# Gate chunks of the second block's modulation computed in the first block's layers

## Chip, cores and metric

One core of a Trainium2 chip runs the whole program. The metric is the device time of one execution in microseconds (us), the median of several runs; less is better.

## What is computed

The reference sends 256 tokens of width 1024 through two layers of a first block (five attention-like branches and an output product each), a final norm, and then one second block. The second block is modulated by a conditioning vector `c`:

```python
def second_block(x, c, w_ada, b_ada, ...):
    c_act = jax.nn.silu(c)
    ada = c_act @ w_ada[l] + b_ada[l]
    shift_a, scale_a, gate_a, shift_m, scale_m, gate_m = jnp.split(ada, N_ADA, axis=-1)
    h = modulate(rmsnorm(x, g_mix[l]), shift_a, scale_a)
    proj = h @ w_in[l]
    ...
    y = jnp.concatenate([o_gla, o_moba], axis=-1) @ w_out[l]
    x = x + gate_a[:, None, :] * y
    h = modulate(rmsnorm(x, g_mlp[l]), shift_m, scale_m)
    x = x + gate_m[:, None, :] * (jnp.square(jax.nn.relu(h @ w_ff1[l])) @ w_ff2[l])
    return rmsnorm(x, g_final)
```

`ada` has 6144 columns, which the kernel computes as 12 chunks of 512: chunks 0 to 3 are shift and scale of the mixers (GLA and MoBA), 4 and 5 the gate `gate_a`, 6 to 9 shift and scale of the MLP, 10 and 11 `gate_m`. They need only `c`, no token.

## The kernel before

All weights are streamed once, in pieces of up to [128, 4, 512] f32 (1 MB). `run_stream` walks the list of pieces: a piece is loaded 6 ahead on SP's queue into one of three raw buffers (L393), split 3 ahead into a rounded high part on ACT (`wh`, L408) and the rest on DVE (`wl`, L409), each with four buffers, and multiplied on TensorE (PE) as three products high × high, low × high, high × low: L470, L471 and L473 for a token-major result, L493, L495 and L496 for a transposed one. The raw buffer is free again when the L409 of its piece has read it.

A chunk of `ada` is two pieces of `w_ada` that are not split (`raw`). DVE alone multiplies and adds them up: for each of the eight rows of the chunk one instruction, L1403 the first and L1405 the other seven, on 128x512. Then `fin` splits the sum (L1414 on ACT, L1415 on DVE), PE sums over partitions with a matrix of ones (L1419, L1420), and either ACT copies one row (L1423), which POOL's queue sends to the array `adaR`, or, for a gate, POOL's queue loads `b_ada` on all partitions (L1430) and DVE adds (L1431). `spread` sorts the chunks' pieces evenly between the other pieces: chunks 0 to 3 in the first layer, 6 to 9 in the second (table `ADA`), 4 and 5 in the second block from its fifth piece on, 10 and 11 in the MLP.

The order on each engine is that of the program, where generators ("lanes") and deferred steps are woven between the chunks of the stream; `behind(mark)` puts an instruction after a marked one, and `tc.high_priority` puts one earlier. Tokens are two tiles of 128, t = 0 and 1, and their 1024 columns two halves, c = 0 and 1. Places that the change and the prediction speak of:

- **start**: `first_x` turns x into an operand (high part L639 on ACT, low part L640 on DVE), and defers the sums of squares `row_stats` (ACT, L694); `warming` works beside it.
- **hand-over** (880 to 906 us): the residual sum of layer 2 (L1247), then `row_norms`: sum of squares (L694), product with the norm's weights in place (L1328), second sum of squares, inverse root on DVE (L247 to L253), the scaled rows (L1358 on DVE, L1359 on ACT), transposes on PE (L612), and `to_operand_mod`: high part on ACT (L654), low part on DVE (L659 and L662; two of eight pieces on ACT, L661). `after_norm` marks two pieces (272 columns each, split in halves of 128x544) whose splits are held: their L409 stand behind the low part of t = 1.
- **mixers** (906 to 1010 us): MoBA in units of 8 L768, 4 L748, 4 L1474 and 6 L612 on PE; for the softmax L718 on DVE and L721 on ACT; ACT's L751 and DVE's L752 bring what L768 wants. GLA works between the units.
- **residual and change-over** (1017 to 1042 us): `eo` for each (t, c): the product with the gate (L1703), the sum (L1704), the sums of squares, then again L1358, transposes and `to_operand_mod` for the MLP; `ff1` (L1830, L1831), whose squares are transposed by L612. L1774 scales the last norm's weights.

Of the kernel before, what the change touches and what calls it, by code (L numbers as in the profile page):

```python
# [9 lines left out]
F32 = mybir.dt.float32  # L10
# [21 lines left out]

ROW = dict(norm=0, memn=16, gmix=24, gmlp=32, bada=40, c=88, qn=96, kvn=102, sgub=106)
NROW = 122
ADA = [(0, 1, 2, 3), (6, 7, 8, 9)]


class Lane:
# [19 lines left out]
def block_kernel(ctx: ExitStack, tc: tile.TileContext, a, out):  # L58
# [86 lines left out]
    def behind(key, on=True):  # L145

        return tc.issue_after(marks[key].ins) if on and key in marks else nullcontext()

    marks = {}
# [225 lines left out]
    def run_stream():  # L375
        W, P = {}, {}
        N = len(pieces)

        def load(i):
            src, nk, n = pieces[i][:3]  # L380
            w = wts.tile([128, 4, 512], F32, tag="w", name=nm("wt"))
            v = w.rearrange("p a b -> p (a b)")[:, :nk * n].rearrange("p (a b) -> p a b", a=nk)
            if i < 2:

                for k in range(0, nk, i + 1):
                    if k == 2 and i:
                        load_x(1)
                    q = A if i == 0 and k < 2 else SY
                    q.dma_start(v[:, k:k + i + 1, :],
                                bass.AP(tensor=src.tensor, offset=src.offset + k * src.ap[1][0],  # L390
                                        ap=[src.ap[0], [src.ap[1][0], i + 1], src.ap[2]]))
            else:
                SY.dma_start(v, src)  # L393
            W[i] = v

        def split(i, by_k=False):
            _, nk, n, fn, _, raw, _ = pieces[i]
            w = W.pop(i)
            if raw:
                fn(w)  # L400
                return
            hi = wts.tile([128, 4, 512], F32R, tag="hi", name=nm("wh"), bufs=LOOK + 1)
            lo = wts.tile([128, 4, 512], F32R, tag="lo", name=nm("wl"), bufs=LOOK + 1)
            hv, lv = (z.rearrange("p a b -> p (a b)")[:, :nk * n] for z in (hi, lo))
            wv = w.rearrange("p a b -> p (a b)")
            def part(k, m, on):
                ks = slice(k * n, min(k + m, nk) * n)
                pin(A.activation(hv[:, ks], wv[:, ks], AF.Copy), on)  # L408
                pin(V.tensor_tensor(lv[:, ks], wv[:, ks], hv[:, ks].bitcast(F32), OP.subtract), on)  # L409

            P[i] = [z.rearrange("p (a b) -> p a b", a=nk) for z in (hv, lv)]
            if by_k:
                return part
            with behind(("lo", 1), id(pieces[i]) in after_norm):
                m = 1 if i == 1 else 2
                for k in range(0, nk, m):
                    part(k, m, pieces[i] in pinned)

        load(0)
        A.activation(small(1), ones[:, 0:1], AF.Copy)  # L420
        load(1)
        first_loads()
        for i in range(2, AHEAD):
            load(i)
        part = split(0, by_k=True)

        def first_x(c, step):
            to_operand_g([x[t][:, c * 512:(c + 1) * 512] for t in range(2)], E["x"][c], 4,
                         lambda i: gcol("norm", 4 * c + i), step)
            for t in range(2):  # L430
                defer(lambda t=t: row_stats(t, c, 0), 1)

        first_x(0, lambda i: part(i, 1, True))
        pinned.extend(pieces[1:LOOK + 1])
        split(1)
        ahead = [2]

        def split_to(i):

            while ahead[0] <= min(i, N - 1) and (ahead[0] < i or id(pieces[ahead[0]]) not in after_norm):  # L440
                split(ahead[0])
                ahead[0] += 1

        def second_x():
            first_x(1, lambda i: None)
            split_to(LOOK)

        defer(second_x, 2)
        for i in range(N):
            if i == 3:  # L450
                load_mem()
                gains_t(1)
                silu_c()
            _, nk, n, fn, pre, raw, late = pieces[i]
            if i > 1 and not late:
                split_to(i + LOOK)
            if i + AHEAD < N:
                load(i + AHEAD)
            if pre:
                pre()  # L460
            if not raw:
                fn(*P.pop(i))
            if late:
                split_to(i + LOOK)
# [181 lines left out]

    def to_operand_mod(src, t, xo, am, bm, k0):

        tmp = work([128, 4, 128])
        hi, lo = xo.hi[:, :, tsl(t)], xo.lo[:, :, tsl(t)]  # L650
        cols = [(am[:, k0 + i:k0 + i + 1], bm[:, k0 + i:k0 + i + 1]) for i in range(4)]
        ps = [transpose4(src[:, b * 256:(b + 1) * 256], 2) for b in range(2)]
        for i, (sc, bi) in enumerate(cols):
            A.activation(hi[:, i, :], ps[i // 2][:, i % 2, :], AF.Identity, scale=sc, bias=bi)  # L654
        for b in range(0, 4, 2):
            for i in range(b, b + 2):
                sc, bi = cols[i]
                if b == 0 or k0 == 0:
                    V.tensor_scalar(tmp[:, i, :], ps[b // 2][:, i - b, :], sc, bi, op0=OP.mult, op1=OP.add)  # L659
                else:  # L660
                    A.activation(tmp[:, i, :], ps[1][:, i - 2, :], AF.Identity, scale=sc, bias=bi)  # L661
            ins = V.tensor_tensor(lo[:, b:b + 2, :], tmp[:, b:b + 2, :], hi[:, b:b + 2, :].bitcast(F32), OP.subtract)  # L662
        if k0 == 0:
            marks["lo", t] = ins

    def stacked(dst, ps):

# [656 lines left out]
    def row_norms(t, c):  # L1324

        hc = x[t][:, c * 512:(c + 1) * 512]
        m = mean_so_far(("m", t), hc, c)
        V.tensor_tensor(hc, hc, B["fg"][:, c * 512:(c + 1) * 512], OP.mult)  # L1328
        if c:
            q = small(1)  # L1330
            V.scalar_tensor_tensor(q, m, RMS_EPS, B["y", t], op0=OP.mult, op1=OP.add)
            B["y", t] = q
        v = mean_so_far(("y", t), hc, c, 0.0)
        if c == 0:
            return
        def back():

            with behind(("lo", 1)):
                V.tensor_scalar(x[t], x[t], rsqrt_scaled(m), SCALED, op0=OP.mult, op1=OP.mult)
        rest = modulated(t, rsqrt_scaled(v), B["x"], B["am"], B["bm"])  # L1340
        for c in range(2):
            defer(lambda c=c: rest(c), 3 - t)
        defer(back, 8 - t)

    def mean_so_far(key, src, c, eps=RMS_EPS):
# [10 lines left out]
    def modulated(t, r, xo, am, bm):  # L1356
        xn = slot([128, D])
        marks["xn", t] = V.tensor_scalar(xn[:, 0:512], x[t][:, 0:512], r, None, op0=OP.mult)  # L1358
        A.activation(xn[:, 512:], x[t][:, 512:], AF.Copy, scale=r)  # L1359

        def rest(c):
            with tc.high_priority(offset=SOONER if c else URGENT + 100):
                to_operand_mod(xn[:, c * 512:(c + 1) * 512], t, xo[c], am, bm, 4 * c)
                xo[c].filled.add(t)
        return rest

    adaT = cst.tile([128, 48], F32, name="adaT")
# [24 lines left out]
    def ada(q, gate=None):  # L1392

        st = {}
        for j in range(2):
# [13 lines left out]
            def fin():  # L1409
# [8 lines left out]
                ps = bbank([128, 512])  # L1418
                T.matmul(ps, ones_r, hi, start=True, stop=False)  # L1419
                T.matmul(ps, ones_r, lo, start=False, stop=True)  # L1420
                if gate is None:
                    row = work([1, 512])
                    A.activation(row, ps[0:1, :], AF.Copy)  # L1423
                    G.dma_start(adaR[q // 6][4 * (q % 6):4 * (q % 6) + 4, :], row)
# [222 lines left out]
    def block2():  # L1647
# [45 lines left out]
        chunk_tr(w2, ops, 1552, eq)  # L1693
        chunk_tr(w2, ops, 2064, ek, post=after_mk)
        chunk(w2, ops, 2576, 512, tok("mv", 512))
        spread(first + 4, [lambda: ada(4, ("ga", 0)), lambda: ada(5, ("ga", 1))])
        chunk(w2, ops, 512, 512, tok("gv", 512), post=lambda: done.add("gv"))
        chunk(w2, ops, 1024, 256, lambda t, ps: silu_into(t, 0, ps), post=lambda: done.add("gr"))

        def residual(t, c, ps, gate):  # L1700
            tmp = work([128, 512])
            cs = slice(c * 512, (c + 1) * 512)
            V.tensor_tensor(tmp, ps, B[gate][:, cs], OP.mult)  # L1703
            marks["res"] = V.tensor_tensor(x[t][:, cs], x[t][:, cs], tmp, OP.add)  # L1704
            v = mean_so_far(("x", t), x[t][:, cs], c)
            if c == 1:
                return rsqrt_scaled(v)

        def eo(c):
            @urgent  # L1710
            def f(t, ps):
# [6 lines left out]
                if c == 1:  # L1718
                    rest = modulated(t, r, B["x2"], B["am"], B["bm"])

                    def second():
                        with behind("res", t == 0):
                            rest(1)
                    defer(lambda: rest(0), 2)
                    defer(second, 3 - t)
            return f
        chunk_pair(a["w_out_2"][0], [lambda: B["xm"], lambda: B["xg"]], [(0, 512), (512, 512)], [eo(0), eo(1)],
                   pres={(0, 0): lambda: run_until("moba"), (1, 0): lambda: run_until("gla")}, rows=(512, 0),
                   by_tile=True, between=lambda: B["second rows"]())

        fo = [lambda: B["x2"][0], lambda: B["x2"][1]]
# [171 lines left out]
```

## Time and profile before

| | before |
|---|---|
| median of 3 runs | 1221.54 us (1221.0 to 1221.8) |
| profiled execution | 1220.62 us |
| its span in the profile | 1218.9 us |
| mean granted TensorE clock | 0.996 |
| busy: PE | 1201.0 us, 99% |
| busy: DVE (VectorE) | 904.1 us, 74% |
| busy: ACT (ScalarE) | 672.5 us, 55% |
| busy: POOL (GpSimd) | 34.0 us, 3% |

Busy shares are means over the span, and PE's ends are modelled; the place of each idle stretch is in the windows and timelines. Times in the views count from the span's start.

### The profile page before, as it was taken

What the parts mean: (1) busy time and instruction counts of PE and PEld (TensorE: products, weight loads), DVE (VectorE), ACT (ScalarE), POOL (GpSimd) and SP (SyncE); (2) the same over time, 40 slices, a digit from 0 to 9 for tenths busy, and PEclk for the clock granted to TensorE, in tenths of its full rate; (3) what the DMA queues carried; (4) which work ended last, traced back from release to release, by engine and by line L of the source; (5) the groups of instructions that cost most, each with busy time, mean ns of one, the idle gap of its engine ahead of it and who ended that gap; (6) DMA issues with size and microseconds to landing.
All of it is one profiled execution on the core that took longest, in us unless ns stands there. A gap on an engine that the chain in (4) does not pass through costs nothing.

```text
span 1218.9 us, 17443 instructions
## 1 busy us (share of the span) xinstructions
PE 1201.0 (99%) x6589; PEld 1039.3 (85%) x6589; DVE 904.1 (74%) x1889; ACT 672.5 (55%) x1188; POOL 34.0 (3%) x68
## 2 busy tenths in 40 slices
PE   9999999999999999999999999999999899999997
PEld 7888988898888888898888988888879787898996
DVE  5996777659886776776877688776788778766755
ACT  5765455547566455546544766654465556545442
POOL 4000000000000000000000000000020010000000
PEclk9999999999999999999999999999999999999999
DMA  9866646454566466655566445655547634666740
GB/s 310 305 230 212 202 141 216 134 175 157 179 210 205 138 219 196 233 174 173 164 221 194 149 151 171 227 190 182 166 138 265 207 114 137 233 218 221 255 145 35
DMA packets 117828, 231.31 MB, mean 190 GB/s; under 512 B 4604, under 2 KB 14496, under 8 KB 117616
## 3 DMA queue, kind: packets, MB, share of 16 engines
q1 hardware_dynamic: 114640, 221.62, 54.6%
q0 software_dynamic: 2640, 7.78, 2.1%
q8 instruction: 52, 0.85, 0.3%
q10 hardware_dynamic: 464, 0.79, 0.2%
q14 instruction: 32, 0.26, 0.1%
HBM read 229.10 MB, written 2.63 MB: 190 GB/s over the span
## 4 chain that ended last, share of the span: by engine, by line
PE 92%; DVE 3%; ACT 2%; DMA 1%; issue 1%; ACTq 0%
PE pm L471 22%; PE pm L470 22%; PE pm L473 22%; PE pm L493 4%; PE pm L495 4%; PE pm L496 4%; PE po L768 3%; PE pm L612 3%; PE pm L748 2%; DMA wt<-in_w_in_dram 1%; PE pm L1164 1%; PE pm L1051 1%; DVE wl L409 1%; ACT j L694 1%; ACT hi L654 1%
## 5 line engine op out<-in xcount | busy, mean ns | idle before, releaser
L409 DVE TENSOR_TENSOR wl<-wt,wh 128x1024 fp32r<-128x1024 f32 (+6 forms) x388 | 443.3, 1170 | 163.6 <-ACT wh L408 162.6
L408 ACT ACTIVATE wh<-wt 128x1024 fp32r<-128x1024 f32 (+6 forms) x388 | 379.6, 1014 | 254.4 <-PE pm L473 141.7
L470 PE MATMUL pm<-wh,hi 128*128 128x512 f32 (+4 forms) x1288 | 500.1, 390 | 0.0
L471 PE MATMUL pm<-wl,hi 128*128 128x512 f32 (+4 forms) x1288 | 490.2, 382 | 0.8 <-DVE wl L409 0.8
L473 PE MATMUL pm<-wh,lo 128*128 128x512 f32 (+4 forms) x1288 | 337.2, 382 | 0.5 <-DVE lo L662 0.5
L471 PEld LDWEIGHTS pm<-wl,hi 128*128 128x128 f32 x1288 | 242.3, 188 | 44.9 <-DVE wl L409 2.1
L470 PEld LDWEIGHTS pm<-wh,hi 128*128 128x128 f32 x1288 | 242.1, 188 | 43.3 <-issue 0.3
L473 PEld LDWEIGHTS pm<-wh,lo 128*128 128x128 f32 x1288 | 237.5, 188 | 47.4 <-DVE lo L662 2.2
L493 PE MATMUL pm<-hi,wh 128*128 128x256 f32 x416 | 118.9, 286 | 0.0
L496 PE MATMUL pm<-hi,wl 128*128 128x256 f32 x416 | 117.7, 283 | 0.0
L495 PE MATMUL pm<-lo,wh 128*128 128x256 f32 x416 | 117.7, 283 | 0.0
L493 PEld LDWEIGHTS pm<-hi,wh 128*128 128x128 f32 x416 | 79.7, 192 | 1.4 <-issue 1.0
L495 PEld LDWEIGHTS pm<-lo,wh 128*128 128x128 f32 x416 | 79.8, 192 | 0.4
L496 PEld LDWEIGHTS pm<-hi,wl 128*128 128x128 f32 x416 | 79.7, 192 | 0.0
L721 ACT ACTIVATE w<-w,s 128x256 f32<-128x256 f32 (+1 forms) x112 | 49.8, 446 | 35.6 <-DVE s L718 35.6
L1405 DVE SCALAR_TENSOR_TENSOR w<-wt,cact,w 128x512 f32<-128x512 f32 x84 | 62.7, 747 | 1.6 <-DMA wt<-in_w_ada_dram 0.6
L768 PEld LDWEIGHTS po<-t,w 128*128 128x128 f32 x352 | 45.9, 191 | 7.0 <-ACT w L751 3.4
L1210 ACT ACTIVATE t<-pm,s 128x512 f32<-128x512 f32 x40 | 27.5, 689 | 40.7 <-PE pm L473 40.6
L768 PE MATMUL po<-t,w 128*128 128x64 f32 (+1 forms) x352 | 45.2, 270 | 3.3 <-ACT w L751 3.0
L612 PE MATMUL pm<-ident,t 128*128 128x128 f32 (+1 forms) x316 | 42.3, 273 | 2.1 <-DVE t L1358 2.0
L612 PEld LDWEIGHTS pm<-ident,t 128*128 128x128 f32 (+1 forms) x316 | 36.8, 138 | 8.5 <-issue 2.2
L694 ACT ACTIVATE j<-t 128x512 f32<-128x512 f32 (+3 forms) x59 | 28.1, 477 | 28.0 <-DVE t L1794 15.7
(318 smaller groups left out, 1043.7 us busy)
## 6 DMA issues: line engine op xcount, KB each, us to landing
wt<-in_w_in_dram SPq DMA_DIRECT2D x96, 1024.0 KB, 5.1
wt<-in_w_ff_dram SPq DMA_DIRECT2D x32, 1024.0 KB, 5.8
wt<-in_w_ada_dram SPq DMA_DIRECT2D x24, 1024.0 KB, 5.2
wt<-in_w_branch_dram SPq DMA_DIRECT2D x20, 1024.0 KB, 5.2
wt<-in_w_out_dram SPq DMA_DIRECT2D x12, 1024.0 KB, 5.2
wt<-in_mem_w_kv_dram SPq DMA_DIRECT2D x8, 1024.0 KB, 5.2
wt<-in_w_in_dram SPq DMA_DIRECT2D x4, 904.0 KB, 4.8
wt<-in_w_in_dram SPq DMA_DIRECT2D x4, 768.0 KB, 4.4
```

The lines of the kernel that those rows point to most:

```text
L408: pin(A.activation(hv[:, ks], wv[:, ks], AF.Copy), on)
L409: pin(V.tensor_tensor(lv[:, ks], wv[:, ks], hv[:, ks].bitcast(F32), OP.subtract), on)
L470: pin(T.matmul(ps[:, :n], xh, hi[:, i, :n], start=first and i == 0, stop=False), on)
L471: pin(T.matmul(ps[:, :n], xh, lo[:, i, :n], start=False, stop=False), on)
L473: ins = pin(T.matmul(ps[:, :n], xo.lo[:, k0 + i, tsl(t)], hi[:, i, :n], start=False, stop=last and i == nk - 1), on)
L493: T.matmul(ps, wh, xh, start=first and i == 0 and c % 2 == 0, stop=False, skip_group_check=True)
L495: T.matmul(ps, wh, xl, start=False, stop=False, skip_group_check=True)
L496: T.matmul(ps, wl, xh, start=False, stop=last and i == nk - 1, skip_group_check=True)
L612: T.transpose(ps[:, i, :], src[:, i * w:(i + 1) * w], ident)
L721: A.activation(p[:, k, :], p[:, k, :], AF.Exp, bias=mx[:, k:k + 1], scale=-1.0, accum_out=sm[:, k:k + 1])
L768: T.matmul(opsum[t][:, h, :], pt[:, k * nb + b, :], u["v"](h, b), start=b == 0, stop=b == nb - 1)
L1405: V.scalar_tensor_tensor(acc, w[:, i, :], B["c"][:, k:k + 1], acc, op0=OP.mult, op1=OP.add)
```

## The change

It does five things.

1. Chunk 4 joins the pieces of the first layer and chunk 5 those of the second (`ADA`), and the `spread` of the second block goes. A gate chunk of `gate_a` now ends in one row: `b_ada` is loaded as one row, added to partition 0 of PE's sum, and stored to an array `garow` in DRAM. Before the first piece of the output product (`output_begins`) POOL's queue loads `garow` to all 128 partitions.
2. `to_operand_mod` issues the high parts and returns a function that issues the low parts. At the residual the low parts of t = 0 are put behind the last product (`mul`), and its second half behind the last sum (`res`).
3. The splits of the held pieces, ACT's L408 too, stand behind the last high part and the last low part of t = 1.
4. `row_norms` writes the product with the norm's weights to a new tile, and not in place.
5. The first half's sums of squares at the start are deferred by three steps, not one.

```diff
-ADA = [(0, 1, 2, 3), (6, 7, 8, 9)]
+ADA = [(0, 1, 2, 3, 4), (6, 7, 8, 9, 5)]
...
-            with behind(("lo", 1), id(pieces[i]) in after_norm):
+            held = id(pieces[i]) in after_norm
+            with behind(("lo", 1), held), behind(("hi", 1), held):
...
-                defer(lambda t=t: row_stats(t, c, 0), 1)
+                defer(lambda t=t: row_stats(t, c, 0), 1 if c else 3)
...
-            A.activation(hi[:, i, :], ps[i // 2][:, i % 2, :], AF.Identity, scale=sc, bias=bi)
...
+            ins = A.activation(hi[:, i, :], ps[i // 2][:, i % 2, :], AF.Identity, scale=sc, bias=bi)
         if k0 == 0:
-            marks["lo", t] = ins
+            marks["hi", t] = ins
+        def low():
+            tmp = work([128, 4, 128])
+            for b in range(0, 4, 2):
...
+            if k0 == 0:
+                marks["lo", t] = lo_ins
+            xo.filled.add(t)
+        return low
...
-        V.tensor_tensor(hc, hc, B["fg"][:, c * 512:(c + 1) * 512], OP.mult)
+        if c == 0:
+            B["h", t] = slot([128, D])
+        yc = B["h", t][:, c * 512:(c + 1) * 512]
+        V.tensor_tensor(yc, hc, B["fg"][:, c * 512:(c + 1) * 512], OP.mult)
...
-        v = mean_so_far(("y", t), hc, c, 0.0)
+        v = mean_so_far(("y", t), yc, c, 0.0)
         if c == 0:
             return
+        x[t] = B["h", t]
...
-            defer(lambda c=c: rest(c), 3 - t)
+            defer(lambda c=c: rest(c)(), 3 - t)
...
-                if gate is None:
+                if q in (4, 5):
+                    row = work([1, 512])
+                    G.dma_start(row, a["b_ada_2"][0:1, q * 512:(q + 1) * 512])
+                    V.tensor_tensor(row, ps[0:1, :], row, OP.add)
+                    if "garow" not in B:
+                        B["garow"] = drm.tile([1, D], F32, name="garow")
+                    G.dma_start(B["garow"][:, csl(q - 4)], row)
+                elif gate is None:
...
-        spread(first + 4, [lambda: ada(4, ("ga", 0)), lambda: ada(5, ("ga", 1))])
...
-            V.tensor_tensor(tmp, ps, B[gate][:, cs], OP.mult)
+            marks["mul"] = V.tensor_tensor(tmp, ps, B[gate][:, cs], OP.mult)
...
+                    low = []
+
                     def second():
+                        with behind("mul", t == 0):
+                            low[0]()
                         with behind("res", t == 0):
-                            rest(1)
-                    defer(lambda: rest(0), 2)
+                            rest(1)()
+                    defer(lambda: low.append(rest(0)), 2)
                     defer(second, 3 - t)
             return f
+        def output_begins():
+            run_until("moba")
+            B["ga"] = slot([128, D])
+            d = B["garow"]
+            G.dma_start(B["ga"], bass.AP(tensor=d.tensor, offset=d.offset, ap=[[0, 128], [1, D]]))
+
         chunk_pair(a["w_out_2"][0], [lambda: B["xm"], lambda: B["xg"]], [(0, 512), (512, 512)], [eo(0), eo(1)],
-                   pres={(0, 0): lambda: run_until("moba"), (1, 0): lambda: run_until("gla")}, rows=(512, 0),
+                   pres={(0, 0): output_begins, (1, 0): lambda: run_until("gla")}, rows=(512, 0),
```

How the order moves, at three places. First DVE's order in the second block, ahead of the first long MoBA unit; in the kernel before (L1405 is a gate chunk's step, L718 the softmax, L409 the weight split, L1559 and L1565 rotate the queries):

```order
1300 L1405 SCALAR_TENSOR_TENSOR w_8783<-wt_8709,cact,w_8783 128x512
1301 L718 ISA w_8986,s_8983<-pm_8980,t_8457 128x256
1302 L718 ISA s_8983 128x1
1303 L1405 SCALAR_TENSOR_TENSOR w_8783<-wt_8709,cact,w_8783 128x512
1304 L718 ISA w_8986,s_8983<-pm_8980,t_8457 128x256
1305 L718 ISA s_8983 128x1
1306 L1559 SCALAR_TENSOR_TENSOR t_8911<-t_8487,w_9000 128x512
1307 L409 TENSOR_TENSOR wl_8946<-wt_8796,wh_8945 128x1024 x2
1308 L729 RECIPROCAL s_8984<-s_8985 128x2
1309 L1565 TENSOR_TENSOR t_8912<-t_8487,w_9003 128x512
1310 L1415 TENSOR_TENSOR w_9008<-w_8783,w_9007 128x512
1311 L409 TENSOR_TENSOR wl_9012<-wt_8858,wh_9011 128x1024 x2
```

The same stretch after the change (its own lines: L727 is L718, L1583 and L1589 are L1559 and L1565):

```order
1311 L409 TENSOR_TENSOR wl_8969<-wt_8755,wh_8968 128x1024
1312 L1583 SCALAR_TENSOR_TENSOR t_8942<-t_8528,w_8961 128x512
1313 L1589 TENSOR_TENSOR t_8943<-t_8528,w_8964 128x512
1314 L409 TENSOR_TENSOR wl_8969<-wt_8755,wh_8968 128x1024
1315 L409 TENSOR_TENSOR wl_9031<-wt_8831,wh_9030 128x512
1316 L727 ISA w_9009,s_9006<-pm_9003,t_8530 128x256
1317 L727 ISA s_9006 128x1
1318 L727 ISA w_9009,s_9006<-pm_9003,t_8530 128x256
1319 L727 ISA s_9006 128x1
1320 L1583 SCALAR_TENSOR_TENSOR t_8942<-t_8528,w_9023 128x512
```

The steps of the gate chunks are gone, and the softmax of the unit stands behind three weight splits.

Second, ACT's order at the hand-over; before (L694 sums of squares of t_87, the first tile, and t_88, the second; L408 the held pieces):

```order
553 L694 ACTIVATE j_8290,s_8288<-t_87 128x512
554 L408 ACTIVATE wh_8467<-wt_8143 128x544
555 L1423 ACTIVATE w_8332<-pm_8329 1x512
556 L694 ACTIVATE j_8320,s_8318<-t_88 128x512
557 L408 ACTIVATE wh_8467<-wt_8143 128x544
558 L1359 ACTIVATE t_8302<-t_87,s_8293 128x512
559 L654 ACTIVATE hi_8244<-pm_8374,adaT,s_8251 128x128 x2
560 L654 ACTIVATE hi_8244<-pm_8377,adaT,s_8251 128x128 x2
561 L694 ACTIVATE j_8326,s_8324<-t_88 128x512
```

After the change (L703 is L694, L1372 is L1359, L655 is L654, L667 is L661), first the same stretch, then the end of the second tile's high parts:

```order
554 L703 ACTIVATE j_8331,s_8329<-t_87 128x512
555 L703 ACTIVATE j_8339,s_8337<-t_8307 128x512
556 L703 ACTIVATE j_8369,s_8367<-t_88 128x512
557 L1372 ACTIVATE t_8351<-t_8307,s_8342 128x512
558 L655 ACTIVATE hi_8292<-pm_8417,adaT,s_8299 128x128 x2
559 L655 ACTIVATE hi_8292<-pm_8420,adaT,s_8299 128x128 x2
560 L703 ACTIVATE j_8376,s_8374<-t_8372 128x512
```

```order
571 L655 ACTIVATE hi_8294<-pm_8484,adaT,s_8299 128x128 x2
572 L655 ACTIVATE hi_8294<-pm_8487,adaT,s_8299 128x128 x2
573 L667 ACTIVATE w_8494<-pm_8487,adaT,s_8299 128x128 x2
574 L408 ACTIVATE wh_8508<-wt_8231 128x544 x2
575 L408 ACTIVATE wh_8565<-wt_8239 128x544 x2
576 L408 ACTIVATE wh_8571<-wt_8277 128x1024 x2
```

The held splits and the row copy no longer stand between the sums of squares; the splits follow the last high part.

Third, DVE's order at the residual; before:

```order
1434 L1358 TENSOR_SCALAR t_9680<-t_87,s_9671 128x512
1435 L1703 TENSOR_TENSOR w_9695<-pm_9538,t_8851 128x512
1436 L1704 TENSOR_TENSOR t_88<-t_88,w_9695 128x512
1437 L659 TENSOR_SCALAR w_9703<-pm_9704,s_9631,adaT 128x128 x2
1438 L659 TENSOR_SCALAR w_9703<-pm_9707,s_9631,adaT 128x128
1439 L662 TENSOR_TENSOR lo_9625<-w_9703,hi_9624 128x2x128
1440 L659 TENSOR_SCALAR w_9703<-pm_9707,s_9631,adaT 128x128
1441 L1352 TENSOR_SCALAR s_9699<-s_9698 128x1
1442 L1703 TENSOR_TENSOR w_9732<-pm_9572,t_8851 128x512
```

After the change (L1371 is L1358, L1726 and L1727 are L1703 and L1704, L665 and L668 are L659 and L662):

```order
1445 L1371 TENSOR_SCALAR t_9688<-t_8307,s_9679 128x512
1446 L1726 TENSOR_TENSOR w_9703<-pm_9546,t_9543 128x512
1447 L1727 TENSOR_TENSOR t_8372<-t_8372,w_9703 128x512
1448 L1726 TENSOR_TENSOR w_9733<-pm_9580,t_9543 128x512
1449 L665 TENSOR_SCALAR w_9753<-pm_9711,s_9639,adaT 128x128 x2
1450 L665 TENSOR_SCALAR w_9753<-pm_9714,s_9639,adaT 128x128
1451 L668 TENSOR_TENSOR lo_9633<-w_9753,hi_9632 128x2x128
1452 L665 TENSOR_SCALAR w_9753<-pm_9714,s_9639,adaT 128x128
1453 L1365 TENSOR_SCALAR s_9707<-s_9706 128x1
1454 L1727 TENSOR_TENSOR t_8372<-t_8372,w_9733 128x512
```

The product of the last residual stands ahead of the first tile's low parts. Some 20 rows on, L1807 (L1774 before) stands ahead of the two splits that precede the first L1864 (L1831 before); in the kernel before it followed six splits later.

## Rows read from the trace of the kernel before

**Rows 1.** The page, part 4: the chain that ended last, by engine

```profile
PE 92%; DVE 3%; ACT 2%; DMA 1%; issue 1%; ACTq 0%
```

**Rows 2.** Windows: us; busy PE, PEld, DVE, ACT, POOL; clock, DMA share, GB/s

```profile
50.00:850.00 800.00, 800.00 (x4267) 692.37 (x4266) 607.74 (x1312) 448.96 (x810) 9.10 (x16) 1.00 0.57 187
...
900.00:950.00 50.00, 48.91 (x338) 44.97 (x338) 42.43 (x84) 27.86 (x45) 2.69 (x7) 1.00 0.66 223
950.00:1000.00 50.00, 46.11 (x280) 37.50 (x279) 33.83 (x113) 29.06 (x77) 4.79 (x9) 0.97 0.52 175
```

**Rows 3.** Waits of PE: us in total, times, the longest

```profile
PE po L768 <- ACT w L751: 3.0, 1, 3.0
PE pm L612 <- DVE t L1358: 2.0, 3, 1.1
...
PE pm L471 <- DVE wl L409: 0.8, 1, 0.8
```

**Rows 4.** Timeline of PE, 955 to 965 us: start, us, what, idle before

```profile
955.09 0.82 PE L473 MATMUL pm<-wh,lo 128*128 128x512 f32 x2
958.88 0.92 PE L768 MATMUL po<-t,w 128*128 128x64 f32 x4 [2.98 <-ACT w L751]
960.07 0.66 PE L768 MATMUL po<-t,w 128*128 128x64 f32 x4 [0.27 <-DVE w L752]
961.15 0.69 PE L748 MATMUL pm<-ident,w 128*128 128x128 f32 x2 [0.42 <-ACT w L721]
...
964.50 0.48 PE L1419 MATMUL pm<-w,onesr 128*128 128x512 f32 x1
```

**Rows 5.** Timeline of PE, 965 to 971 us

```profile
967.78 1.00 PE L768 MATMUL po<-t,w 128*128 128x64 f32 x8
...
970.50 0.48 PE L470 MATMUL pm<-wh,hi 128*128 128x512 f32 x1
```

**Rows 6.** Windows of 10 and 5 us in the second block

```profile
910.00:920.00 10.00, 10.00 (x84) 10.00 (x83) 9.51 (x24) 3.16 (x7) 0.00 (x0) 1.00 0.96 332
...
960.00:965.00 5.00, 4.51 (x20) 3.76 (x21) 3.60 (x18) 2.41 (x8) 0.00 (x0) 0.66 0.98 362
```

**Rows 7.** Timeline of ACT, 950 to 961 us

```profile
955.03 3.04 ACT L408 ACTIVATE wh<-wt 128x1024 fp32r<-128x1024 f32 x4 [0.25 <-DMA wt<-in_w_in_dram]
...
958.46 0.37 ACT L751 ACTIVATE w<-pm 128x256 f32<-128x256 f32 x1
```

**Rows 8.** Groups of DVE by form: busy, mean ns of one, idle before

```profile
L1405 DVE SCALAR_TENSOR_TENSOR w<-wt,cact,w 128x512 f32<-128x512 f32 x84 | 62.7, 747 | 1.6 <-DMA wt<-in_w_ada_dram 0.6
```

**Rows 9.** Timelines of DVE and PE, 790 to 806 us, second layer

```profile
800.13 1.21 DVE L409 TENSOR_TENSOR wl<-wt,wh 128x1024 fp32r<-128x1024 f32 x1
...
805.24 0.39 PE L471 MATMUL pm<-wl,hi 128*128 128x512 f32 x1
```

**Rows 10.** Timeline of POOL's queue, 986 to 992 us

```profile
987.49 0.54 POOL L1773 DMA_DIRECT2D t<-in_g_final_dram  x1
```

**Rows 11.** The view of DMA issues: queue, count, KB each, us to landing

```profile
t<-in_g_final_dram POOLq DMA_DIRECT2D x1, 512.0 KB, 5.0
```

**Rows 12.** Timeline of DVE, 1016 to 1050 us

```profile
1017.21 0.68 DVE L1703 TENSOR_TENSOR w<-pm,t 128x512 f32<-128x512 f32 x1
...
1039.94 0.68 DVE L1831 SCALAR_TENSOR_TENSOR w<-pm,w 128x512 f32<-128x512 f32 x1
...
1049.40 0.68 DVE L1774 TENSOR_SCALAR t<-t 128x1024 f32<-128x1024 f32 x1
```

**Rows 13.** Timeline of ACT at the hand-over

```profile
891.16 0.64 ACT L408 ACTIVATE wh<-wt 128x544 fp32r<-128x544 f32 x1
891.71 0.57 ACT L1423 ACTIVATE w<-pm 1x512 f32<-1x512 f32 x1
```

**Rows 14.** Timeline of DVE at the start

```profile
15.25 0.54 DVE L266 CAST posf<-posi 2x128 f32<-2x128 int32 x1
16.29 0.48 DVE L640 SCALAR_TENSOR_TENSOR lo<-pm,gT,hi 128x256 fp32r<-128x256 f32 x1 [0.50 <-ACT hi L639]
```

More of the change, by code (lines that the diff above doesn't have):

```diff
@@ L647, in to_operand_mod @@
     def to_operand_mod(src, t, xo, am, bm, k0):
-        tmp = work([128, 4, 128])
         hi, lo = xo.hi[:, :, tsl(t)], xo.lo[:, :, tsl(t)]
@@ L653, in to_operand_mod @@
         for i, (sc, bi) in enumerate(cols):
-            A.activation(hi[:, i, :], ps[i // 2][:, i % 2, :], AF.Identity, scale=sc, bias=bi)
[L655 to L662, printed above, removed]
-        if k0 == 0:
-            marks["lo", t] = ins
+            ins = A.activation(hi[:, i, :], ps[i // 2][:, i % 2, :], AF.Identity, scale=sc, bias=bi)
+        if k0 == 0:
+            marks["hi", t] = ins
+        def low():
+            tmp = work([128, 4, 128])
+            for b in range(0, 4, 2):
+                for i in range(b, b + 2):
+                    sc, bi = cols[i]
+                    if b == 0 or k0 == 0:
+                        V.tensor_scalar(tmp[:, i, :], ps[b // 2][:, i - b, :], sc, bi, op0=OP.mult, op1=OP.add)
+                    else:
+                        A.activation(tmp[:, i, :], ps[1][:, i - 2, :], AF.Identity, scale=sc, bias=bi)
+                lo_ins = V.tensor_tensor(lo[:, b:b + 2, :], tmp[:, b:b + 2, :], hi[:, b:b + 2, :].bitcast(F32),
+                                         OP.subtract)
+            if k0 == 0:
+                marks["lo", t] = lo_ins
+            xo.filled.add(t)
+        return low
     def stacked(dst, ps):
@@ L1361, in rest, with prior, g @@
         def rest(c):
-            with tc.high_priority(offset=SOONER if c else URGENT + 100):
-                to_operand_mod(xn[:, c * 512:(c + 1) * 512], t, xo[c], am, bm, 4 * c)
-                xo[c].filled.add(t)
+            def prior(f):
+                def g(*args):
+                    with tc.high_priority(offset=SOONER if c else URGENT + 100):
+                        return f(*args)
+                return g
+            return prior(prior(to_operand_mod)(xn[:, c * 512:(c + 1) * 512], t, xo[c], am, bm, 4 * c))
         return rest
```

## Prediction

> **What bounds the kernel now.** I began with the chain of waits on the page: TensorE holds 92% of it [rows 1], so what the change does to the other engines counts only where TensorE waits for them. The table of windows says where that is: from 50 to 850 us PE is busy for all of 800 us, while from 900 to 950 it lacks 1.09 us and from 950 to 1000 3.89 us [rows 2]. These are the second block's start and its mixers. PE's own list of waits names the places: one wait of 3.0 us of an L768 for ACT's L751, three of together 2.0 us (the longest 1.1) of the transposes L612 for DVE's L1358, one of 0.8 us of L471 for DVE's L409 [rows 3].
>
> The largest place has to be read by its length and not by its idle time. In the timeline of PE the unit of MoBA work (8 L768, 4 L748, 4 L1474, 6 L612) should begin at 955.55, when the two L473 of 955.09 are through at 0.23 each; L1419, which follows the unit, begins at 964.50 [rows 4]: 8.95 us. The next unit of the same instructions runs from 967.78 to 970.50 [rows 5]: 2.72 us. So 6.2 us are lost, of which the waits shown are 2.98, 0.27 and 0.42 [rows 4], 3.7 in all. The other 2.5 us are work at a lower pace: the granted clock from 960 to 965 is 0.66 of full speed [rows 6], a mean of stretches at 1.2 and at 2.4 GHz.
>
> Why it stalls: ACT's L751 runs at 958.46, behind four weight splits L408 of 3.04 us, which had themselves waited for their weights [rows 7]. These came late because the three raw buffers are emptied by DVE, and DVE had 9.51 of 10 us of work from 910 on, with the DMA engines at 0.96 of their time and 332 GB/s [rows 6]. The gate chunks are part of both: on DVE eight instructions of at most 0.75 us for one chunk [rows 8], 12.0 us for two, with their splits and sums on top; and 4 MB of weights, 12.6 us at 332 GB/s.
>
> **The change, part by part.**
>
> Gate chunks out of the second block. Over 12.0 us of DVE and 12.6 us of DMA leave the stretch from 910 to 965 us; the 6.2 us lost are less than either. Without L1405 between them, the L409 that free the raw buffers run earlier, so do the loads, and the four L408 no longer stand as a block ahead of L751. Next late there is the unit's own chain (scores, L718, L721, L748). It made PE wait 0.42 us at 961.15 [rows 4], but not at all in the unit at 967.78 [rows 5]; I count it as covered. Bounds: 3.7 us if only the waits go, 6.2 if all goes. I take −6.2, since that is the pace of the very next unit. The Trainium skill, in TensorE: Matmul & The Clock Gate, section HAM oscillation — how this bites in real kernels, says that a long wait of TensorE lowers its clock and is paid again in the matmuls behind it; by that rule both parts of the loss go together, without it only the idle part would, and the sum would come out at 1217.6. The trace agrees with the rule: the stretch with the shorter waits, 900 to 950, kept a clock of 1.00 [rows 2].
>
> Gate chunks into the layers. PE has no wait to lose there, but DVE gets 6.0 us more for a chunk, once in each layer. The cover is the lead of the splits: the piece whose split ends at 801.34 is used at 805.24 [rows 9], 3.9 us, the shortest lead between 55 and 880 us; most are over 10. A chunk comes as two pieces of four instructions, apart from each other in the stream, so 3.0 us of DVE meet 3.9 of lead: 0. Bound: a whole chunk against the shortest lead, 6.0 − 3.9 = 2.1. Its two matmuls cost PE the same wherever they stand. The gate row's two small DMAs and its add on one partition have hundreds of us before they are needed. The broadcast of the finished row stands on POOL's queue behind the GLA norm weights and ahead of the final norm's load, which was issued at 987.49 and whose 512 KB landed after 5.0 us [rows 10, 11]; the first use is the residual at 1017.21 [rows 12]: over 20 us of cover. POOL's loads for the GLA gates now stand behind the garow store, which waits for DVE's add just after the hand-over; before, they were there well ahead of their use. I count 0.
>
> Hand-over (880 to 906 us). The weight splits of 544 columns and the copy L1423 leave ACT's queue ahead of the second tile's sums: one L408 of 0.64 and the L1423 of 0.57 stood on the way [rows 13], so the second tile's transposes can start 1.2 us earlier, where they had waited 1.1 [rows 3]. One pair of ones matmuls moves behind them (0.46, as the two L473 of rows 4): −0.7. Bounds 0 (DVE's statistics set the end anyway) and −1.1. The held splits come after the last high part now; by their durations they are ready about 1 us before their first use. The norm product in another tile takes away its wait for the sum of squares and adds no instruction.
>
> Start. The first two sums of squares leave ACT's queue ahead of the high parts of x, which may begin earlier; the low part, at 16.29, is then bound by DVE, whose cast ends at 15.79 [rows 14]: −0.5, bounds 0 and the wait of L471, −0.8 [rows 3].
>
> Change-over to the MLP (1017 to 1042 us). Two things go against it. The product of the last residual now stands ahead of the first tile's low parts and waits for PE, so that the second tile's sum and L1358 come about 0.3 us later; and L1774, 0.68 us, stands ahead of the two L409 that precede L1831, whose end at 1040.62 released PE [rows 12]. For it, ACT loses two held splits between the sums. I take +1.0 (0.3 + 0.7). Bounds: −0.9, if the two other waits for L1358 vanish (2.0 less 1.1 [rows 3]), and +2.0, if the second L1831 is late, too, by a held split of 1.0 us on ACT.
>
> **The sum.** −0.5 − 0.7 − 6.2 + 1.0 = −6.4 us against the profiled execution of 1220.6: 1214.2. The median of the runs before lies 0.9 above that execution; in the same measure the forecast is **1215.1**.
>
> **The rivals.**
> A, a new wait replaces part of the stall: the unit's own chain L718, L721, L748, or the next 1 MB of weights. If only the idle part comes back (3.7 of 6.2): 1217.6; if a wait of 1 us is left beside that: 1218.6. For it: DVE is near its limit before 950 even with 6 us less; against it: the next unit without a wait.
> B, the change-over does what moving the low parts could do, −0.9 in place of +1.0: 1213.2. For it: ACT free of held splits between the sums; against it: L1774 and the wait in DVE's order.
> C, the stall has nothing to do with the gate chunks: the loads of in_w_in alone keep it (ACT waited for a DMA at 955.03 [rows 7]). Then −0.5 − 0.7 + 1.0 = −0.2: 1221.3. Against it: 4 MB less on DMA engines that ran at 0.96.
> D, slower: in the layers the added DVE work comes out on PE. Place: the stretches where DVE has no free time; price: at most the whole 12.0 us, 1227.1. It makes the kernel slower only from 8.9 us on (1215.1 + 8.9 = 1224.0), so both chunks would have to find nearly no lead. Against it: PE busy for 800 of 800 us beside a DVE busy for 608 of them [rows 2].
>
> **How the numbers follow.** Forecast 0.60, A 0.17, B 0.12, C 0.07, D 0.04. Some 0.2% (2.4 us) is what a measurement of this kernel can tell from no change: faster is below 1219.1. That takes the forecast, B, and most of A (0.14): 0.86 faster; C and the rest of A, 0.10, the same; 0.04 slower. The range begins where the bounds that gain lie together (−0.8 − 1.1 − 6.2 − 0.9 = −9.0: 1212.5) and reaches over A to 1219.0; C, D and the tail of A are left out, and with them some 0.15.
>
> **What would show it.** In the changed profile: no wait of 3 us of the L768 for ACT, and a granted clock of 1.00 around 960; the MoBA units there all of about 2.7 us; PE busy for all of 50 to 850; the second tile's transposes at the hand-over without their 1.1 us; a wait of about 1.5 us ahead of the first transposes of the MLP's squares. A wait of the first residual for the broadcast gate, or idle PE in a layer behind an L409, would prove the forecast wrong, and so would a stall of over 2 us left in the mixers.

## The result

The changed kernel takes 1232.51 us (median of 4 runs, 1232.12 to 1232.73) against 1221.55 us before: a ratio of 1.009 with a 95% interval of 1.0073 to 1.0108, 11 us slower. The forecast was 1215.1 us with a range to 1219.0, so it was wrong in its sign. The profiled execution has a span of 1231.0 us against 1218.9. One execution of the experiments, the profiled one of the kernel with parts 3 and 4 undone, took 3817 us; it is in no number here.

The stall in the mixers did go, as forecast. The windows of the changed kernel at the times of [rows 2], with the columns of that group (the last two hold work that the kernel before did 11 to 18 us earlier):

```profile
50.00:850.00 800.00, 790.08 (x4191) 683.40 (x4191) 609.02 (x1315) 442.62 (x802) 10.64 (x19) 0.99 0.57 187
...
900.00:950.00 50.00, 48.16 (x297) 42.14 (x296) 40.03 (x95) 33.81 (x66) 3.46 (x6) 1.00 0.50 165
950.00:1000.00 50.00, 50.00 (x326) 44.33 (x325) 29.68 (x90) 29.75 (x69) 4.27 (x8) 1.00 0.39 126
```

PE is busy for all of 950 to 1000, where 3.89 us were missing; the stall's work, at 955 to 965 us before, lies in this window too. The loss is in the first line: from 50 to 850, where PE had been busy for 800 of 800 us, it now lacks 9.92 us. PE's list of waits, which answers to [rows 3], has new names at its head:

```profile
PE pm L471 <- ACT hi L627: 4.3, 2, 3.4
PE po L777 <- ACT w L760: 2.4, 2, 2.0
PE po L777 <- DVE w L761: 1.7, 2, 0.9
...
PE pm L474 <- DVE lo L668: 1.1, 3, 0.6
PE pm L613 <- DVE w L1864: 1.1, 1, 1.1
PE pm L1550 <- DVE w L1545: 1.0, 1, 1.0
PE pm L613 <- DVE t L320: 0.9, 1, 0.9
```

L777 and L760 are L768 and L751 of before (the softmax attention's product and what it waits for), L627 is L626, the high part of a branch's output. All of these but those of L474, of L613 for L1864 and of L1550 lie in the layers. The wait of L1550, in the GLA part of the second block, is new; in the two traces of one and the same kernel of the first experiment it is 0.7 us long and absent, so it comes and goes.

To see how much each place costs I compared the two traces piece by piece: when does PE make the first product of the same weight piece? The changed kernel is ahead by 0.5 us at 194 us; behind by 5.7 at 256 us; by 5.4 at 556; by 10.0 at 595; by 11.6 at 797; by 18.5 at 853; and by 12.0 at 1041 (times of the kernel before). So about 6 us are lost near 205 us, 4.5 near 580, over 1 near 750 and 7 near 820, 19 in all, and the second block gives back 6.5: the distance falls from 18.0 us at 940 to 11.2 at 960, where the stall was. Some 1 us of the 19 is no loss, since the two moved chunks' own matmuls now stand in the layers: the own-lane kernel below, which has no wait there, goes from 0.8 us ahead at 194 us to 0.5 behind at 853.

The timeline of PE in the changed kernel at the first place (start, duration, what, idle before):

```profile
205.37 0.39 PE L1436 MATMUL pm<-w,onesr 128*128 128x512 f32 x1
205.60 0.39 PE L1437 MATMUL pm<-w,onesr 128*128 128x512 f32 x1
205.83 0.60 PE L757 MATMUL pm<-ident,w 128*128 128x128 f32 x4
206.19 0.36 PE L687 MATMUL pm<-t,t 128*128 128x256 f32 x1
206.38 0.28 PE L688 MATMUL pm<-t,t 128*128 128x256 f32 x1
206.50 0.28 PE L687 MATMUL pm<-t,t 128*128 128x256 f32 x1
206.62 0.28 PE L688 MATMUL pm<-t,t 128*128 128x256 f32 x1
208.93 0.66 PE L777 MATMUL po<-t,w 128*128 128x64 f32 x4 [2.03 <-ACT w L760]
210.45 0.66 PE L777 MATMUL po<-t,w 128*128 128x64 f32 x4 [0.86 <-DVE w L761]
211.42 0.69 PE L757 MATMUL pm<-ident,w 128*128 128x128 f32 x2 [0.31 <-ACT w L730]
```

and the same attention step in the kernel before (L748 is L757, L768 is L777):

```profile
208.69 0.60 PE L748 MATMUL pm<-ident,w 128*128 128x128 f32 x4
...
211.44 1.07 PE L473 MATMUL pm<-wh,lo 128*128 128x512 f32 x4
...
214.16 1.07 PE L473 MATMUL pm<-wh,lo 128*128 128x512 f32 x4
215.07 1.00 PE L768 MATMUL po<-t,w 128*128 128x64 f32 x8
```

Before, two blocks of weight products (each ending in four L473) stand between the transposed probabilities and the product that needs them back from ACT and DVE. After, nothing stands there, and PE waits out the round trip. Right ahead of the place are L1436 and L1437, the sum of a modulation chunk. At the second place, too, that pair stands at 582.63. After the transposes of 584.08 PE waits from 585.12 on, until ACT's high part of a branch's output has come. Of the third and fourth place one wait each follows:

```profile
582.63 0.48 PE L1436 MATMUL pm<-w,onesr 128*128 128x512 f32 x1
...
584.08 1.04 PE L613 MATMUL pm<-ident,t 128*128 128x128 f32 x8
588.48 0.50 PE L471 MATMUL pm<-wh,hi 128*128 128x512 f32 x1 [3.36 <-ACT hi L627]
...
751.81 0.50 PE L471 MATMUL pm<-wh,hi 128*128 128x512 f32 x1 [0.92 <-ACT hi L627]
...
821.16 0.66 PE L777 MATMUL po<-t,w 128*128 128x64 f32 x4 [0.85 <-DVE w L761]
```

**Why the order changed.** The closing steps of a chunk (`fin`) and those of a branch's output (`og`) are generators in one lane, `lanes[2]`, first in, first out, one step for each piece of the stream; a `fin` takes six. Before a branch's product, `run_until(key)` steps all three lanes until `og` has finished. With four chunks in a layer, no `og` was ever late: counting the steps of `run_until` while the program is written gives none for all ten branches. With five, all chunks lie at other places between the pieces, and five branches find `og` unfinished, four of them with a `fin` ahead of it. The loop then writes out, with no weight product between, two steps of the DSA attention and one of the MLA attention in the first layer, and three steps of DSA's preparation, two of the differential and three of the MLA attention in the second. Four of these five are the places of loss above; the one MLA step of the first layer costs nothing that the comparison shows. PE loses in two ways: attention steps follow each other bare (the waits of L777), and the branch's product follows bare on the steps that make its own operand (the waits of L471 for L627). That is the theory of the order. The rival is the one that the forecast named for a slower kernel: the added DVE work in the layers comes out on PE.

### The profile page after: what moved, and what is told of

Same layout as the page of the kernel before. It is cut to its first block, busy times and chain, and to the rows that moved or that the text cites. A ratio compares the mean times of both kernels' runs of the same rounds, so it can differ in the third digit from the quotient of the medians.

```text
span 1231.0 us, 17461 instructions
## 1 busy us (share of the span) xinstructions
PE 1206.4 (98%) x6589; PEld 1045.6 (85%) x6589; DVE 906.6 (74%) x1889; ACT 673.7 (55%) x1188; POOL 36.5 (3%) x71
## 4 chain that ended last, share of the span: by engine, by line
PE 75%; DVE 5%; ACT 1%; DMA 1%; issue 1%; ACTq 0%
PE pm L471 18%; PE pm L472 18%; PE pm L474 18%; PE pm L494 3%; PE pm L497 3%; PE pm L496 3%; PE po L777 2%; PE pm L613 2%; PE pm L757 1%; DVE wl L409 1%; PE pm L1173 1%; PE pm L1060 1%; DMA wt<-in_w_in_dram 1%; PE po L474 1%; PE po L472 1%
## 5 line engine op out<-in xcount | busy, mean ns | idle before, releaser
L409 DVE TENSOR_TENSOR wl<-wt,wh 128x1024 fp32r<-128x1024 f32 (+6 forms) x388 | 444.9, 1171 | 181.6 <-ACT wh L408 181.1
L408 ACT ACTIVATE wh<-wt 128x1024 fp32r<-128x1024 f32 (+6 forms) x388 | 379.4, 1016 | 272.8 <-PE pm L474 152.9
L471 PE MATMUL pm<-wh,hi 128*128 128x512 f32 (+4 forms) x1288 | 499.8, 389 | 4.3 <-ACT hi L627 4.3
L474 PE MATMUL pm<-wh,lo 128*128 128x512 f32 (+4 forms) x1288 | 337.0, 382 | 1.3 <-DVE lo L668 1.1
L471 PEld LDWEIGHTS pm<-wh,hi 128*128 128x128 f32 x1288 | 242.1, 188 | 47.6 <-ACT hi L627 4.7
L474 PEld LDWEIGHTS pm<-wh,lo 128*128 128x128 f32 x1288 | 237.5, 188 | 48.7 <-DVE lo L668 3.4
L777 PEld LDWEIGHTS po<-t,w 128*128 128x128 f32 x352 | 46.9, 194 | 7.8 <-ACT w L760 3.0
L777 PE MATMUL po<-t,w 128*128 128x64 f32 (+1 forms) x352 | 46.5, 273 | 4.1 <-ACT w L760 2.4
L613 PE MATMUL pm<-ident,t 128*128 128x128 f32 (+1 forms) x316 | 43.1, 278 | 1.7 <-DVE t L320 0.9
L613 PEld LDWEIGHTS pm<-ident,t 128*128 128x128 f32 (+1 forms) x316 | 37.6, 141 | 7.4 <-DVE t L1371 1.8
L703 ACT ACTIVATE j<-t 128x512 f32<-128x512 f32 (+3 forms) x59 | 28.3, 479 | 28.4 <-DVE t L1827 15.7
```

Of the source, the lines that this page charges most:

```text
L471: pin(T.matmul(ps[:, :n], xh, hi[:, i, :n], start=first and i == 0, stop=False), on)
L474: ins = pin(T.matmul(ps[:, :n], xo.lo[:, k0 + i, tsl(t)], hi[:, i, :n], start=False, stop=last and i == nk - 1), on)
L613: T.transpose(ps[:, i, :], src[:, i * w:(i + 1) * w], ident)
L777: T.matmul(opsum[t][:, h, :], pt[:, k * nb + b, :], u["v"](h, b), start=b == 0, stop=b == nb - 1)
```

## The experiments

Times are medians; each ratio is against runs of the kernel before on the same chip, with its 95% interval.

### The closing steps in a lane of their own

```diff
-    lanes = [Lane(), Lane(), Lane()]
+    lanes = [Lane(), Lane(), Lane(), Lane()]
...
-            moved = [ln.step() for ln in lanes]
+            moved = [ln.step() for ln in (lanes if name[0] == "ada" else lanes[:3])]
...
             lanes[2].step()
+            lanes[3].step()
...
-                    lanes[2].add(fin())
+                    lanes[3].add(fin())
```

> The changed kernel, but the closing steps of the modulation chunks (fin) step in a lane of their own, not in the lane in which the branches' normalised outputs (og) queue; all other work is the same. Theory of the order: the 11 us came from five places where a branch's product ran the lanes empty because og stood behind a fin, so that attention steps follow each other on PE without weight products between them; without them the layers are full again and what is left is the forecast of the second block: 1214 to 1217 us, PE busy for all of 50 to 850. Rival, DVE load: the two added chunks cost DVE the same here, so the time stays at 1231 to 1233.

1214.75 us, ratio 0.9949 (0.9934 to 0.9964); repeated with the kernels further down, 1214.56 us, 0.9945 (0.9932 to 0.9957), for which I had expected:

> The own-lane kernel once more, beside the three that differ from it in one place: 1214.2 to 1215.3.

The windows of the first of the two:

```profile
50.00:850.00 800.00, 799.91 (x4265) 691.80 (x4264) 615.28 (x1324) 450.05 (x812) 11.42 (x20) 1.00 0.58 192
...
50.00:450.00 400.00, 400.00 (x2178) 347.50 (x2177) 307.66 (x650) 225.99 (x401) 5.42 (x10) 1.00 0.58 194
450.00:870.00 420.00, 419.91 (x2184) 361.04 (x2184) 324.35 (x696) 233.41 (x423) 6.76 (x11) 1.00 0.58 193
950.00:1000.00 50.00, 49.83 (x313) 41.66 (x313) 31.83 (x116) 27.01 (x74) 5.34 (x10) 1.00 0.40 128
```

The layers are full again with all the added DVE work in them, and the time is that of the forecast. 17.8 us of the changed kernel are due to the shared lane.

### Without the added DVE work

```diff
-                    else:
+                    elif q not in (4, 5):
                         V.scalar_tensor_tensor(acc, w[:, i, :], ...)
```

Seven of the eight DVE steps of chunks 4 and 5 are left out; their loads, their closing steps and the order stay.

> The changed kernel, with seven of the eight DVE steps of chunks 4 and 5 left out (the gate is then computed from one eighth of its rows); loads, fin and order stay. Theory of the order: unchanged, 1230 to 1233. Rival, DVE load in the layers: 10.5 us less for DVE where it is needed, 1213 to 1218.

1234.71 us, ratio 1.0107 (1.0091 to 1.0124): not faster than the changed kernel, whose interval it overlaps. PE's waits are the same ones:

```profile
PE pm L471 <- ACT hi L627: 4.3, 2, 3.4
PE po L777 <- ACT w L760: 2.4, 2, 2.0
PE pm L613 <- DVE t L320: 1.9, 1, 1.9
PE po L777 <- DVE w L761: 1.7, 2, 0.9
```

The DVE load is not the cause.

### Half of the places

In the own-lane kernel, the own lane for the chunks of one layer only: `lanes[3 if q in ADA[0] else 2].add(fin())`, and `ADA[1]` for the other half.

> As the run with the own lane, but only for the chunks of the first layer (0 to 4); those of the second layer (5 to 9) stay in og's lane. Theory of the order: the two places of the first layer go (5.9 us by the traces), the three of the second stay: 1226 to 1228. If the own lane helped for another reason (fin earlier or later in general), nearer to 1215.

> The other half: own lane for the chunks of the second layer and after, those of the first in og's lane. Theory of the order: the two places of the first layer stay (5.9 us on 1214.8), those of the second go: 1220 to 1222.

1227.89 us (1.0046, 1.0035 to 1.0058; ten executions from 1222.05 to 1229.21) and 1220.02 us (0.999, 0.9981 to 1.0; ten from 1218.65 to 1223.11). Counted as above, the first keeps the three places of the second layer and the second the two of the first. The windows show that, of the first kernel and then of the second:

```profile
50.00:450.00 400.00, 400.00 (x2178) 347.55 (x2177) 307.72 (x649) 226.81 (x402) 5.42 (x10) 1.00 0.58 195
450.00:870.00 420.00, 413.01 (x2123) 354.69 (x2122) 317.64 (x686) 229.12 (x417) 5.98 (x10) 0.99 0.55 184
```

```profile
50.00:450.00 400.00, 396.80 (x2151) 344.95 (x2150) 301.77 (x642) 222.06 (x396) 4.33 (x8) 1.00 0.57 191
450.00:870.00 420.00, 419.91 (x2185) 361.05 (x2184) 324.35 (x695) 233.56 (x423) 7.89 (x13) 1.00 0.57 193
```

Against the changed kernel's 1232.51 they save 4.6 and 12.5 us, 17.1 together, where both at once saved 17.8: the places add up.

### A late output without any move

In the kernel before, no chunk moved:

```diff
             def og():
+                for _ in range(3):
+                    yield
```

> The kernel before, with og waiting three more steps of its lane: no chunk is moved and no instruction is added. Theory of the order: og comes too late at two branch products of the second layer, whose lanes are then run empty (three steps of dsa_prep, two of mla_attn); at the price of the changed kernel's places of the same kind (5.9 us for three steps of dsa_prep, about 5 for two of mla_attn) 1229 to 1233. Rival, DVE load: 1221 to 1222.

1241.11 us, ratio 1.0164 (1.0148 to 1.0179). Slower, as the order alone should make it, but by 8 us more than I had expected. Its list of waits shows what I had left out:

```profile
PE pm L470 <- ACT hi L626: 8.3, 7, 2.3
PE po L768 <- ACT w L751: 4.2, 1, 4.2
```

Seven products wait for the high part of their own branch's output: a late `og` costs PE also where `run_until` finds it done, since its operand is not ready. The edit is therefore no clean measure of the emptied lanes alone; it shows that the order makes the loss with no DVE work and no load added.

### The first part undone

The gate chunks go back to the second block (`ADA`, `spread`, the gate on all partitions as before); the other four parts of the change stay.

> The changed kernel with its first part undone: the gate chunks are again in the second block, with the gate on all partitions; the other four parts stay. By the forecast's terms: start -0.5, hand-over -0.7 and change-over +1.0, and the stall of 6.2 us in the mixers stays: 1221 to 1222. If the stall had to do with the held splits or the tile, it goes here already: 1215 to 1217.

1220.99 us, ratio 1.0002 (0.9992 to 1.0011). The wait of 2.9 us of L777 for L760 in the mixers is there as before:

```profile
PE po L777 <- ACT w L760: 2.9, 1, 2.9
```

With the own-lane kernel this puts 6.2 us (1220.99 − 1214.75) on the move of the chunks, as the forecast had it.

### Is the mixers' stall made by DVE or by the loads?

The kernel before, with the same edit as in the second experiment: the chunks' loads stay, seven of eight of their DVE steps go.

> The kernel before, with seven of the eight DVE steps of chunks 4 and 5 left out (the gate is computed from one eighth of its rows); their 4 MB are still loaded, and fin stays. If DVE's load makes the stall of the mixers: 1214.5 to 1216, the stall gone. If the loads make it (the rival that the chunks' transfers fill the queues): 1220.5 to 1222.

1216.07 us, ratio 0.9954 (0.9939 to 0.9969). Two of its windows:

```profile
910.00:920.00 10.00, 10.00 (x82) 9.96 (x82) 7.83 (x23) 3.41 (x7) 0.00 (x0) 1.00 0.95 325
950.00:1000.00 50.00, 49.31 (x310) 41.15 (x310) 34.92 (x118) 30.05 (x83) 4.80 (x9) 1.00 0.47 151
```

The DMA engines are as full as before (0.95, 325 GB/s, against 0.96 and 332 in [rows 6]), DVE falls from 9.51 to 7.83 us of 10, and the stall is gone: 5.4 us. The 4 MB without DVE's steps do not make it. That the steps would make it without the loads is not shown: no run leaves out the loads alone.

### The smaller parts

Three kernels from the own-lane kernel. In the first, the residual's low parts are issued at once:

```diff
-                        with behind("mul", t == 0):
-                            low[0]()
...
-                    defer(lambda: low.append(rest(0)), 2)
+                    defer(lambda: rest(0)(), 2)
```

> The own-lane kernel with the residual's part of change 2 undone: the first tile's low parts are issued with its high parts, and not behind the last product. By the forecast's term for the order at the change-over (0.3 of the 1.0 us), and by the two new waits of the own-lane run for a low part there (0.26 and 0.58 us): these two waits go, 1213.9 to 1214.7. If the moved low parts help as meant, 1215 to 1216.

1213.40 us, ratio 0.9934 (0.9922 to 0.9946), the lowest median of all. The two waits for a low part are gone from the change-over; the wait of the transposes of the squares stays at 1.15 us:

```profile
1033.13 0.66 PE L614 MATMUL pm<-ident,w 128*128 128x128 f32 x4 [1.15 <-DVE w L1861]
```

The second kernel also holds the scaling of the last norm's weights:

```diff
-                        V.tensor_scalar(B["gf"], B["gf"], SCALED, None, op0=OP.mult)
+                        with behind("sq"):
+                            V.tensor_scalar(B["gf"], B["gf"], SCALED, None, op0=OP.mult)
...
+            marks["sq"] = V.scalar_tensor_tensor(sq, ps, 0.0, r, op0=OP.max, op1=OP.mult)
```

> As the run before it, and the scaling of the last norm's weights held behind the first squares of the MLP, which takes 0.68 us of DVE from ahead of the two splits. By the other 0.7 us of the forecast's term: the wait ahead of the squares' transposes falls from 1.15 to about 0.5 us, 1213.2 to 1214.2; the fastest so far. If the two splits wait for ACT in any case: no gain.

1213.70 us, ratio 0.9936 (0.9923 to 0.9948): no gain on the first that the medians can tell. The wait falls from 1.15 to 0.82 us and not to 0.5, since the two splits then wait for ACT, in the timelines of DVE and PE:

```profile
1031.52 2.36 DVE L410 TENSOR_TENSOR wl<-wt,wh 128x1024 fp32r<-128x1024 f32 x2 [0.18 <-ACT wh L409]
```

```profile
1034.53 0.66 PE L614 MATMUL pm<-ident,w 128*128 128x128 f32 x4 [0.82 <-DVE w L1862]
```

The third undoes parts 3 and 4, the held ACT splits and the tile of the norm's product (`yc = hc`, no `behind(("hi", 1))`).

> The own-lane kernel with changes 3 and 4 undone: the held pieces' ACT splits no longer behind the high parts, and the norm's product in place. By the forecast's term for the hand-over (-0.7, bounds 0 and -1.1): 1215.2 to 1216, with the wait of the second tile's transposes back at about 1 us. If these two parts do nothing: 1214.5 to 1215.

1214.31 us (median of five), ratio 0.9939 (0.9926 to 0.9953), nothing lost against the own-lane kernel's 1214.56. No waits of this kernel are read here.

### The move and the lane alone

The kernel before with part 1 and the own lane, without the other four parts.

> The kernel before with the first part of the change alone (chunks 4 and 5 in the layers, the gate as one row) and the lane of their own for fin; the other four parts are not made. If the whole gain over the kernel before is the stall of the mixers: 1213.5 to 1215.5, the same as the own-lane kernel, and parts 2 to 5 are worth nothing together. If the hand-over, the start and the change-over have the forecast's terms (together -0.2): no difference from that either; a clear loss against the own-lane kernel (1216 or more) would show that one of the four parts is needed.

1214.19 us, ratio 0.9945 (0.9931 to 0.9958): the same as with them. The waits at its hand-over and change-over, in the timelines of PE:

```profile
902.78 1.09 PE L613 MATMUL pm<-ident,t 128*128 128x128 f32 x8 [0.50 <-DVE t L1359]
```

```profile
1026.62 1.09 PE L613 MATMUL pm<-ident,t 128*128 128x128 f32 x8 [0.69 <-DVE t L1359]
1030.40 0.73 PE L474 MATMUL pm<-wh,lo 128*128 128x512 f32 x2 [0.22 <-DVE lo L663]
1034.41 0.66 PE L613 MATMUL pm<-ident,w 128*128 128x128 f32 x4 [0.53 <-DVE w L1844]
```

At the hand-over the wait is 0.50 us where it was 1.1 [rows 3]. In the changed kernel, with parts 3 and 4, it is 0.54, and with those parts but without the move (the kernel with the first part undone) 0.77, first line and second:

```profile
919.25 1.09 PE L613 MATMUL pm<-ident,t 128*128 128x128 f32 x8 [0.54 <-DVE t L1371]
```

```profile
901.67 1.06 PE L613 MATMUL pm<-ident,t 128*128 128x128 f32 x8 [0.77 <-DVE t L1371]
```

So those parts shorten it by some 0.3 us alone, the move (with its lane) does as much as both together, and beside the move the parts add nothing to it.

## Why the prediction was wrong, step by step

- **Gate chunks into the layers: 0, at most 2.1.** This step failed; in its place the runs show 17.8 us, the time that the own lane gave back (1232.51 to 1214.75). I priced the added DVE work against the lead of the splits, and that price was right: the own-lane kernel does the same work and PE is busy for 799.9 of 800 us. What I did not follow is the queue in which the chunks' closing steps stand. The diff shows only two numbers in a table; the step behind the number is that all chunks of a layer, old ones too, move against the branches' outputs in a first-in, first-out lane, and that somebody waits for that lane. "Its two matmuls cost PE the same wherever they stand" was true of the two matmuls and false of what follows them. The order of the changed kernel on PE has attention steps without products between them; the orders that I worked from are those of DVE and ACT, at the three places where I expected something.
- **Rival D** had the sign and the layers, but the wrong mechanism and so the wrong bound and chance. Its place, stretches where DVE has no free time, was wrong too: in the windows of the losses DVE is busy for 5.40 to 6.47 us of 10 (last section). Taking the DVE work away changed nothing (1234.7), while taking the order away brought all of it back. That it came to more than the 12.0 us of D fits that.
- **Gate chunks out of the second block: −6.2.** Right, 6.2 us between the kernel with the chunks left in place and the own-lane kernel. Of the two causes that I gave, DVE's steps are shown to be needed, and the loads do not make the stall without them; so rival C falls, too. The pace went with the waits: the granted clock of 950 to 1000 is 1.00 instead of 0.97. Where the Trainium skill (TensorE: Matmul & The Clock Gate, section HAM oscillation — how this bites in real kernels) has the matmuls behind a long wait start at the low clock, this part agrees: the waits and the slow work went together. The length of a wait alone does not tell when the clock falls here: the waits in the layers differ, as the last section shows.
- **Hand-over: −0.7.** The wait fell from 1.09 to 0.54 us, so half a microsecond. Parts 3 and 4, which I gave as the reason, bring it to 0.77 alone, but the move and its lane bring it to 0.50 without them; beside the move they have no share that the runs can tell from none.
- **Change-over: +1.0.** Right in sign and place: the wait of the squares' transposes grew from 0.56 to 1.11 us, two waits for low parts of 0.26 and 0.58 came, and one of 0.70 went. That sums to some 0.7 us; low parts at once are 1.2 us faster in the medians (1213.4 against 1214.6). The intervals of the two ratios overlap, but the five executions of each do not (1212.93 to 1214.24 and 1214.31 to 1216.19).
- **Start: −0.5.** Not shown. The changed kernel was ahead by 0.5 us at 194 us, and the wait of L471 for L409 is gone. But that wait is gone in the move-and-lane kernel, too, which lacks this part and is no slower in the median, and the kernel with the first part undone, which has it, is 0.2 us behind the kernel before at 194 us. PE's first wait for x itself, which differs between the traces (0.5 us before, 0.9 in the changed kernel, 1.1 in those two), hides a term of this size.
- **The sum** of the parts without the failed step, 1215.1, is 0.4 to 0.5 us from the own-lane kernel's two medians. That bears out the −6.2. The three small terms sum to −0.2, and the kernel with the parts behind them alone shows no change (1.0002); that they fit as a sum does not show each of them.

## What to carry to other kernels

When work is moved into a stretch that is full on the bound engine, free time on the other engines is only half of the question: ask which queue its later steps enter, who waits for that queue, and what is written out while it is emptied. A wait in the program text costs nothing in its own lines; it takes away the filler that stood between two dependent steps on PE. A move of the same work into a queue of its own turned 11 us lost into 7 won here.

## What the runs showed that I had not expected

The cost of a wait in clock was not in the order of its length. A single wait of 3.36 us at 588 left the granted clock at 1.00, while waits of 2.03 and 0.86 us with little between them at 209 came with a window of 0.83, and three waits of together 1.5 us at 820 with one of 0.66 (both are means of stretches at 1.2 and 2.4 GHz). The windows of the changed kernel:

```profile
210.00:220.00 10.00, 9.23 (x51) 8.50 (x52) 6.04 (x25) 3.92 (x12) 0.00 (x0) 0.83 0.33 105
580.00:590.00 10.00, 6.64 (x42) 5.65 (x41) 6.47 (x11) 6.78 (x13) 0.53 (x1) 1.00 0.39 117
590.00:600.00 10.00, 10.00 (x46) 8.26 (x45) 9.80 (x25) 2.28 (x3) 0.00 (x0) 1.00 0.54 191
...
820.00:830.00 10.00, 8.83 (x49) 8.56 (x49) 5.40 (x28) 4.24 (x20) 1.07 (x2) 0.66 0.34 107
```

What decides it stays open; so a place has to be priced by the length of the work and not by the waits shown, as at [rows 4].
